# A hybrid decoder layer in split fp32r products: the moving operand read from two halves in turn

## The chip, the cores and the metric

The kernel runs on one core of a Trainium2 chip. A core has a matrix engine (TensorE, PE in the profile, with its weight loads as PEld), a vector engine (VectorE, DVE), a scalar engine (ScalarE, ACT), GpSimd (POOL) and SyncE (SP), which here only issues transfers. Operands lie in SBUF, 128 partitions wide; TensorE writes its sums to PSUM, in banks of 128 x 512 float32. The metric is the device time of one execution in microseconds (us); lower is better.

## The reference

One layer on 256 tokens of width 2048, in float32: a SwiGLU feed-forward block, a mixer with gated linear attention and dilated attention, and a second feed-forward block.

```python
x = x + 0.5 * swiglu(rms_norm(x, ffn1_norm), w_gate, w_up, w_down)        # d_ff = 5632
z = rms_norm(x, mix_norm) @ w_in                                          # split among the head groups
o_g = gla_chunked(...)        # 4 heads, chunks of 64, low-rank forget gate, rms norm and silu gate
o_a = dilated_attention(...)  # 8 heads of 128, three causal dilated windows, merged by softmax
x = x + concat(o_g, o_a) @ w_out
x = x + 0.5 * swiglu(rms_norm(x, ffn2_norm), w_gate2, w_up2, w_down2)

def swiglu(x, w_gate, w_up, w_down):
    return (silu(x @ w_gate) * (x @ w_up)) @ w_down
```

Nearly all the arithmetic is in the dense products with the weights: 2048 x 11264 and 5632 x 2048 twice, 2048 x 6160 for the mixer's input, 2048 x 2048 for its output.

## The kernel before

Each dense product is worked in *column pairs*: two blocks of 512 output columns (`j` = 0, 1) for both halves of the tokens (`t` = 0, 1), so four sums, each in one PSUM bank (`acc`, 6 banks). The loop in `column_pair` goes over the inner dimension in steps `k` of 128. In a step the activations are the stationary operand (128 x 128, loaded anew for each product) and a weight tile of 128 x 512 is the moving operand, which streams through the array.

Weights come from HBM as tiles of 1 MB (`raw`, issued on SP's queue, L148), two steps in each. `split` (L89, L90) turns a step's 128 x 1024 weights into two fp32r tiles: ScalarE writes the rounded value `wh`, VectorE the remainder `wl`. Activations are kept in such halves as well (`hh`/`hl` for the normed input, `uh`/`ul` for the hidden layer, `oah`/`oal` and `ogh`/`ogl` for the mixer's output). `products` then adds three products for each `t` and `j`: high x high (L164), high x low (L166), low x high (L168). A weight step is thus read by 12 products. Four buffers each of `wh` and `wl` are there; ScalarE may overwrite one when the products that read it have ended.

After the last step, `evac(t, ps)` reads the two banks of a token half out of PSUM. In the feed-forward blocks this is a Silu with a per-token scale on ScalarE (`sg`, L218) and a multiplication on VectorE (`u`, L219); `u` is then transposed on TensorE (L85, into a `tp` bank) and split into `uh` and `ul`. The down products and the mixer's output add into the residual `xs` on VectorE (L234, L557), after which the norm of the next part follows in pieces (`norm_block`, `stat_block`), taken from the list `later` and strewn among the next column pair's steps. The mixer's input columns are copied out by ScalarE (L346, L472, L473, L544). The low-rank gate (`gate_low`, L425 to L427) has products of 256 columns of its own and doesn't use `products`. The order on each engine is set by the framework's scheduler from the order of the program.

Transposes, the attention and the gated linear attention run between the steps of column pairs.

Of the kernel before, what the change touches and what calls it, by code (L numbers as in the profile page):

```python
# [17 lines left out]
AF = mybir.ActivationFunctionType  # L18
ALU = mybir.AluOpType
# [17 lines left out]
def layer_kernel(tc, x, xT, gains, gla_gate_up, gla_gate_bias, gla_out_norm, att_q_norm, att_k_norm,  # L37
                 w_ff1, w_dn1, w_mix, w_low, w_out, w_ff2, w_dn2, c_sq, c_rope, c_mask, out):

    nc = tc.nc  # L40
# [3 lines left out]
    with ExitStack() as es:  # L44
# [5 lines left out]
        def acc_bank():  # L50
            return pacc.tile([P, 512], F32, name="acc", tag="acc")

        def t512(name):
            return cst.tile([P, 512], F32, name=name, tag="t512", bufs=4)

        def tp_bank():
            return ptp.tile([P, 512], F32, name="tp", tag="tp")
# [10 lines left out]
        rt = cst.tile([P, NT], F32, name="rt")  # L68
        rq = cst.tile([P, 48], F32, name="rq")[:, :NT]
# [13 lines left out]
        def transpose(dst, src):  # L83
            n = src.shape[0]
            nc.tensor.transpose(dst, src, ident[:n, :n])  # L85

        def split(dst_h, dst_l, src):

            nc.scalar.activation(dst_h, src, AF.Copy)  # L89
            nc.vector.tensor_sub(dst_l, src, dst_h.bitcast(F32))  # L90
# [62 lines left out]
        def weights():  # L153
            while jobs and len(ready) <= AHEAD:
                prepare()
            return ready.pop(0)

        def products(ps, t, acts, ws, first, last, js=((0, 1),)):
            for jj in js:
                for i, ((ah, al, k), (wh, wl)) in enumerate(zip(acts, ws)):  # L160
                    sh = ah[:, k, t * P:(t + 1) * P]
                    sl = al[:, k, t * P:(t + 1) * P]
                    for j in jj:
                        nc.tensor.matmul(ps[j], lhsT=sh, rhs=wh[:, j, :], start=first and i == 0, stop=False)  # L164
                    for j in jj:
                        nc.tensor.matmul(ps[j], lhsT=sh, rhs=wl[:, j, :], start=False, stop=False)  # L166
                    for j in jj:
                        nc.tensor.matmul(ps[j], lhsT=sl, rhs=wh[:, j, :], start=False, stop=last and i == len(ws) - 1)  # L168

        later = []  # L170

        def run_later(n):
            for _ in range(min(n, len(later))):
                later.pop(0)()

        def column_pair(acts, evac, span=28, due=None, extra=None, final=False):

            ps = [None] * NT
            n = len(acts)
            total = done = 0
            i = 0
            while i < n:
                if i == due:
                    done += len(later)
                    run_later(len(later))
                if extra and i in extra:  # L190
                    extra[i]()
                g = WBUF if final and i == n - WBUF else 1
                ws = [weights() for _ in range(g)]
                for t in range(NT):
                    step = 2 * i + t
                    total = max(total, done + len(later))
                    go = max(-(-total * min(step + 1, span) // span) - done, 0)
                    done += min(go, len(later))
                    run_later(go)
                    if i == 0:  # L200
                        ps[t] = [acc_bank(), acc_bank()]
                    last = i + g == n
                    products(ps[t], t, acts[i:i + g], ws, i == 0, last, ((0,), (1,)) if g > 1 else ((0, 1),))
                    if last:
                        evac(t, ps[t])
                i += g

        hacts = [(hh, hl, k) for k in range(KT)]
# [2 lines left out]
        def ffn(name, done, extra=None, final=False):  # L211
            with tc.tile_pool(name=name, bufs=1, reuse_waits="tile") as fp:
                uh = fp.tile([P, FT, S], F32R, name="uh")
                ul = fp.tile([P, FT, S], F32R, name="ul")
                for b in range(FF // 512):
                    def evac(t, ps, b=b):
                        sg, u = t512("sg"), t512("u")
                        nc.scalar.activation(sg, ps[0], AF.Silu, scale=rt[:, t:t + 1])  # L218
                        nc.vector.scalar_tensor_tensor(u, ps[1], rt[:, t:t + 1], sg, op0=ALU.mult, op1=ALU.mult)  # L219
                        tb = tp_bank()  # L220
                        for j in range(4):
                            transpose(tb[:, j * P:(j + 1) * P], u[:, j * P:(j + 1) * P])
                        split(uh[:, 4 * b:4 * b + 4, t * P:(t + 1) * P], ul[:, 4 * b:4 * b + 4, t * P:(t + 1) * P],
                              tb.rearrange("p (j q) -> p j q", j=4))
                    if b:
                        column_pair(hacts, evac)
                    else:
                        column_pair(hacts, evac, span=16, due=15 if extra else 8, extra=extra)
                for cp in range(2):
                    def evac(t, ps, cp=cp):  # L230
                        for j in range(2):
                            c = 2 * cp + j
                            blk = xs[:, t, c * 512:(c + 1) * 512]
                            nc.vector.scalar_tensor_tensor(blk, ps[j], 0.5, blk, op0=ALU.mult, op1=ALU.add)  # L234
                            done(t, c, blk)
                    column_pair([(uh, ul, k) for k in range(FT)], evac, final=final and cp == 1)

# [19 lines left out]
        def renorm(t, c, gi):  # L257

            later.append(lambda: norm_block(t, c, gi))
            later.append(lambda: stat_block(t, c))  # L260
            if c == 3:
                later.append(lambda: norm_finish(t))
# [8 lines left out]
        with tc.tile_pool(name="mix", bufs=1, reuse_waits="tile") as mp:  # L271
# [69 lines left out]
            def store(dst, after=None):  # L341

                def f(t, ps):
                    for j in range(2):
                        blk = dst[:, t, j * 512:(j + 1) * 512]
                        nc.scalar.activation(blk, ps[j], AF.Copy, scale=rt[:, t:t + 1])  # L346
                        if after:
                            later.append(lambda blk=blk, j=j: after(t, j, blk))
                return f
# [63 lines left out]
            def t4k(name):  # L413
                return mp.tile([P, NT, 512], F32, name=name, tag=name, bufs=1)

            qg, kg, la, e1, e2, e3 = (t4k(n) for n in ("qg", "kg", "la", "e1", "e2", "e3"))
# [52 lines left out]
                nc.vector.tensor_mul(kg[:, t, :], kg[:, t, :], er)  # L469

            def evac_qk(t, ps):
                nc.scalar.activation(qg[:, t, :], ps[0], AF.Copy, scale=rq[:, t:t + 1])  # L472
                nc.scalar.activation(kg[:, t, :], ps[1], AF.Copy, scale=rt[:, t:t + 1])  # L473

            column_pair(hacts, evac_qk, span=32)

            vg, on = big("vg"), big("on")
# [53 lines left out]
            def gated(t, j, sg):  # L531
                v = lambda a: a.rearrange("p (h d) -> p h d", h=2)
                nc.vector.tensor_mul(v(sg), v(sg), gon.unsqueeze(1).to_broadcast([P, 2, GDV]))
                nc.vector.tensor_mul(sg, sg, onv[:, t, j * 512:(j + 1) * 512])
                tb = tp_bank()
                for i in range(4):
                    transpose(tb[:, i * P:(i + 1) * P], sg[:, i * P:(i + 1) * P])
                split(oghv[:, 4 * j:4 * j + 4, t * P:(t + 1) * P], oglv[:, 4 * j:4 * j + 4, t * P:(t + 1) * P],
                      tb.rearrange("p (j q) -> p j q", j=4))

            def evac_r(t, ps):
                for j in range(2):
                    sg = t512("sg")
                    nc.scalar.activation(sg, ps[j], AF.Silu, scale=rt[:, t:t + 1])  # L544
                    later.append(lambda j=j, sg=sg: gated(t, j, sg))

            for h in range(GH):
                later.append(lambda h=h: gla_head(h))
            column_pair(hacts, evac_r)

            oacts = [(oah, oal, k) for k in range(8)] + [(oghv, oglv, k) for k in range(8)]
            for cp in range(2):
                def evac(t, ps, cp=cp):
                    for j in range(2):
                        c = 2 * cp + j
                        blk = xs[:, t, c * 512:(c + 1) * 512]
                        nc.vector.tensor_add(blk, blk, ps[j])  # L557
                        renorm(t, c, 2)
                column_pair(oacts, evac, span=4, due=8 if cp == 0 else None)

# [80 lines left out]
```

## Time and profile before

| | |
|---|---|
| median of 3 runs | 1882.87 us (1882.58 to 1882.98) |
| profiled execution | 1883.92 us, its span 1882.0 us |
| TensorE busy | 1871.7 us (99%), 8462 products and transposes |
| TensorE weight loads | 1542.8 us (82%), beside the products |
| VectorE busy | 971.8 us (52%) |
| ScalarE busy | 844.1 us (45%) |
| GpSimd busy | 28.3 us (2%) |
| DMA | 353.79 MB, mean 188 GB/s |
| mean granted TensorE clock | 0.998 |

A group row of the profile reads: line, engine, operation, result<-operands, shapes (partitions x elements per partition), count | busy us, mean ns of one | idle time of the engine before them and what ended it. A row in order of time reads: start, duration (of all that are merged into the row), engine, line, operation, and in brackets the idle time before it. A row of waits reads: who waited for whom, us in total, times, the longest. A row by stretch gives the window, then for each engine its busy time with the number of instructions, then the granted clock and the DMA's share and rate. Products overlap in the array, so the duration of one is longer than the distance between the starts of two.

### The profile page before, as it was taken

What the parts mean: (1) busy time and instruction counts of PE and PEld (TensorE: products, weight loads), DVE (VectorE), ACT (ScalarE), POOL (GpSimd) and SP (SyncE); (2) the same over time, 40 slices, a digit from 0 to 9 for tenths busy, and PEclk for the clock granted to TensorE, in tenths of its full rate; (3) what the DMA queues carried; (4) which work ended last, traced back from release to release, by engine and by line L of the source; (5) the groups of instructions that cost most, each with busy time, mean ns of one, the idle gap of its engine ahead of it and who ended that gap; (6) DMA issues with size and microseconds to landing.
All of it is one profiled execution on the core that took longest, in us unless ns stands there. A gap on an engine that the chain in (4) does not pass through costs nothing.

```text
span 1882.0 us, 20806 instructions
## 1 busy us (share of the span) xinstructions
PE 1871.7 (99%) x8462; PEld 1542.8 (82%) x8462; DVE 971.8 (52%) x998; ACT 844.1 (45%) x1012; POOL 28.3 (2%) x34
## 2 busy tenths in 40 slices
PE   8999999999999999999999999999999999999999
PEld 7888888888888888888887788888888888888887
DVE  5444544554444545566655555444444544544543
ACT  6444444444433434554753444444444444443332
POOL 0000000000000001011000000000000000000000
PEclk9999999999999999999999999999999999999999
DMA  8555555555555555555444355555555555555653
GB/s 314 185 196 182 198 180 199 180 182 198 191 190 200 179 201 196 187 193 185 157 157 149 142 179 187 193 184 196 181 199 180 200 181 197 182 200 183 221 198 115
DMA packets 52111, 353.79 MB, mean 188 GB/s; under 512 B 5904, under 2 KB 7952, under 8 KB 9776
## 3 DMA queue, kind: packets, MB, share of 16 engines
q1 hardware_dynamic: 48672, 348.15, 51.6%
q10 hardware_dynamic: 2896, 3.17, 0.5%
q0 software_dynamic: 448, 1.15, 0.2%
q8 instruction: 66, 1.08, 0.2%
q14 instruction: 29, 0.24, 0.0%
HBM read 350.35 MB, written 2.10 MB: 187 GB/s over the span
## 4 chain that ended last, share of the span: by engine, by line
PE 99%; ACT 1%; DMA 0%; issue 0%; DVE 0%; ACTq 0%
PE acc L164 32%; PE acc L168 32%; PE acc L166 32%; PE tp L85 2%; PE tp L505 0%; DMA xt<-in_xT_dram 0%; PE tp L371 0%; PE tp L520 0%; PE tp L523 0%; ACT wh L89 0%; ACT L438 0%; PE acc L427 0%; PE acc L426 0%; PE acc L425 0%; PE tp L434 0%
## 5 line engine op out<-in xcount | busy, mean ns | idle before, releaser
L90 DVE TENSOR_TENSOR wl<-raw,wh 128x1024 fp32r<-128x1024 f32 x658 | 803.6, 1225 | 765.6 <-ACT wh L89 765.1
L89 ACT ACTIVATE wh<-raw 128x1024 fp32r<-128x1024 f32 x658 | 694.7, 1060 | 862.5 <-PE acc L168 852.7
L166 PE MATMUL acc<-wl,hh 128*128 128x512 f32 x1792 | 568.7, 392 | 0.0
L168 PE MATMUL acc<-wh,hl 128*128 128x512 f32 x1792 | 563.3, 391 | 0.0
L164 PE MATMUL acc<-wh,hh 128*128 128x512 f32 x1792 | 558.0, 392 | 4.4 <-ACT wh L89 4.4
L164 PEld LDWEIGHTS acc<-wh,hh 128*128 128x128 f32 x1792 | 336.7, 188 | 74.7 <-ACT wh L89 4.7
L168 PEld LDWEIGHTS acc<-wh,hl 128*128 128x128 f32 x1792 | 336.3, 188 | 71.3 <-issue 2.1
L166 PEld LDWEIGHTS acc<-wl,hh 128*128 128x128 f32 x1792 | 336.3, 188 | 70.6 <-issue 2.0
L166 PE MATMUL acc<-wl,uh 128*128 128x512 f32 x704 | 220.0, 389 | 0.0
L168 PE MATMUL acc<-wh,ul 128*128 128x512 f32 x704 | 219.1, 389 | 0.0
L164 PE MATMUL acc<-wh,uh 128*128 128x512 f32 x704 | 218.3, 390 | 0.0
L166 PEld LDWEIGHTS acc<-wl,uh 128*128 128x128 f32 x704 | 132.1, 188 | 27.4
L168 PEld LDWEIGHTS acc<-wh,ul 128*128 128x128 f32 x704 | 132.1, 188 | 27.3
L164 PEld LDWEIGHTS acc<-wh,uh 128*128 128x128 f32 x704 | 132.1, 188 | 27.3
L90 DVE TENSOR_TENSOR ul<-tp,uh 128x512 fp32r<-128x512 f32 x44 | 30.0, 691 | 69.5 <-ACT uh L89 69.5
L89 ACT ACTIVATE uh<-tp 128x512 fp32r<-128x512 f32 x44 | 26.3, 599 | 84.9 <-PE tp L85 83.3
L218 ACT ACTIVATE sg<-acc,rt 128x512 f32<-128x512 f32 x44 | 30.4, 690 | 16.4 <-PE acc L168 14.7
L219 DVE SCALAR_TENSOR_TENSOR u<-acc,rt,sg 128x512 f32<-128x512 f32 x44 | 32.9, 748 | 5.3 <-ACT sg L218 5.3
L85 PE MATMUL tp<-ident,u 128*128 128x128 f32 x176 | 26.4, 272 | 0.0
L85 PEld LDWEIGHTS tp<-ident,u 128*128 128x128 f32 x176 | 21.9, 141 | 4.4
L106 POOL TENSOR_TENSOR rs<-a,mhalf 128x4 f32<-128x4 f32 (+1 forms) x12 | 17.5, 1455 | 292.2 <-DVE a L321 292.2
L164 PE MATMUL acc<-wh,oah 128*128 128x512 f32 x64 | 21.0, 396 | 0.0
(147 smaller groups left out, 561.8 us busy)
## 6 DMA issues: line engine op xcount, KB each, us to landing
raw<-in_w_ff_dram SPq DMA_DIRECT2D x175, 1024.0 KB, 4.8
raw<-in_w_dn_dram SPq DMA_DIRECT2D x88, 1024.0 KB, 4.7
raw<-in_w_mix_dram SPq DMA_DIRECT2D x48, 1024.0 KB, 4.8
raw<-in_w_out_dram SPq DMA_DIRECT2D x16, 1024.0 KB, 4.8
xt<-in_xT_dram ACTq DMA_DIRECT2D x8, 256.0 KB, 8.0
xs<-in_x_dram SPq DMA_DIRECT2D x2, 1024.0 KB, 9.8
raw<-in_w_ff_dram SPq DMA_DIRECT2D x4, 256.0 KB, 5.8
raw<-in_w_low_dram SPq DMA_DIRECT2D x1, 1024.0 KB, 4.8
```

Source lines behind the costliest of these rows:

```text
L85: nc.tensor.transpose(dst, src, ident[:n, :n])
L89: nc.scalar.activation(dst_h, src, AF.Copy)
L90: nc.vector.tensor_sub(dst_l, src, dst_h.bitcast(F32))
L106: nc.gpsimd.tensor_tensor(dst, src, mhalf[:, :src.shape[-1]], op=ALU.pow)
L164: nc.tensor.matmul(ps[j], lhsT=sh, rhs=wh[:, j, :], start=first and i == 0, stop=False)
L166: nc.tensor.matmul(ps[j], lhsT=sh, rhs=wl[:, j, :], start=False, stop=False)
L168: nc.tensor.matmul(ps[j], lhsT=sl, rhs=wh[:, j, :], start=False, stop=last and i == len(ws) - 1)
L218: nc.scalar.activation(sg, ps[0], AF.Silu, scale=rt[:, t:t + 1])
L219: nc.vector.scalar_tensor_tensor(u, ps[1], rt[:, t:t + 1], sg, op0=ALU.mult, op1=ALU.mult)
```

## The change

Two helpers give other views of the same memory. `alt` lets the 512 columns of a weight tile be read as column 0, 256, 1, 257, ..., 255, 511. The sums therefore stand in PSUM in that order, written one after the other as before. Where they are read out, `column_pair` hands the evacuation each bank in a view that takes the even words first and then the odd ones (2 runs of 256 with a step of two), and `halves` gives the result the matching two runs, which follow one another, so that every result lies where it did. The weight splits, the transfers, the stationary operands, the gate's 256-column products, the transposes and the order of the instructions on each engine are the same; lines behind the helpers have numbers higher by 7 (L164 is L171, L166 is L173, L168 is L175, L218 is L225, L219 is L226).

```diff
+        def alt(a):
+
+            return a.rearrange("p (b a) -> p a b", b=2)
+
+        def halves(a):
+            return a.rearrange("p (b a) -> p b a", b=2)
+
         def products(ps, t, acts, ws, first, last, js=((0, 1),)):
...
                     for j in jj:
-                        nc.tensor.matmul(ps[j], lhsT=sh, rhs=wh[:, j, :], start=first and i == 0, stop=False)
+                        nc.tensor.matmul(ps[j], lhsT=sh, rhs=alt(wh[:, j, :]), start=first and i == 0, stop=False)
                     for j in jj:
-                        nc.tensor.matmul(ps[j], lhsT=sh, rhs=wl[:, j, :], start=False, stop=False)
+                        nc.tensor.matmul(ps[j], lhsT=sh, rhs=alt(wl[:, j, :]), start=False, stop=False)
                     for j in jj:
-                        nc.tensor.matmul(ps[j], lhsT=sl, rhs=wh[:, j, :], start=False, stop=last and i == len(ws) - 1)
+                        nc.tensor.matmul(ps[j], lhsT=sl, rhs=alt(wh[:, j, :]), start=False, stop=last and i == len(ws) - 1)
...
                     if last:
-                        evac(t, ps[t])
+                        evac(t, [b.rearrange("p (a b) -> p b a", b=2) for b in ps[t]])
...
-                        nc.scalar.activation(sg, ps[0], AF.Silu, scale=rt[:, t:t + 1])
-                        nc.vector.scalar_tensor_tensor(u, ps[1], rt[:, t:t + 1], sg, op0=ALU.mult, op1=ALU.mult)
+                        nc.scalar.activation(halves(sg), ps[0], AF.Silu, scale=rt[:, t:t + 1])
+                        nc.vector.scalar_tensor_tensor(halves(u), ps[1], rt[:, t:t + 1], halves(sg), op0=ALU.mult, op1=ALU.mult)
...
-                            nc.vector.scalar_tensor_tensor(blk, ps[j], 0.5, blk, op0=ALU.mult, op1=ALU.add)
+                            nc.vector.scalar_tensor_tensor(halves(blk), ps[j], 0.5, halves(blk), op0=ALU.mult, op1=ALU.add)
...
-                        nc.vector.tensor_add(blk, blk, ps[j])
+                        nc.vector.tensor_add(halves(blk), halves(blk), ps[j])
```

The other evacuations (L346, L472, L473, L544) take `halves` in the same way.

More of the change, by code (lines that the diff above doesn't have):

```diff
@@ L345, in f @@
                         blk = dst[:, t, j * 512:(j + 1) * 512]
-                        nc.scalar.activation(blk, ps[j], AF.Copy, scale=rt[:, t:t + 1])
+                        nc.scalar.activation(halves(blk), ps[j], AF.Copy, scale=rt[:, t:t + 1])
                         if after:
@@ L471, in evac_qk @@
             def evac_qk(t, ps):
-                nc.scalar.activation(qg[:, t, :], ps[0], AF.Copy, scale=rq[:, t:t + 1])
-                nc.scalar.activation(kg[:, t, :], ps[1], AF.Copy, scale=rt[:, t:t + 1])
+                nc.scalar.activation(halves(qg[:, t, :]), ps[0], AF.Copy, scale=rq[:, t:t + 1])
+                nc.scalar.activation(halves(kg[:, t, :]), ps[1], AF.Copy, scale=rt[:, t:t + 1])
             column_pair(hacts, evac_qk, span=32)
@@ L543, in evac_r @@
                     sg = t512("sg")
-                    nc.scalar.activation(sg, ps[j], AF.Silu, scale=rt[:, t:t + 1])
+                    nc.scalar.activation(halves(sg), ps[j], AF.Silu, scale=rt[:, t:t + 1])
                     later.append(lambda j=j, sg=sg: gated(t, j, sg))
```

## The prediction

> **What bounds the kernel now.** I read the head of the page first, then the chain that ended last, then the stretches in time, then the costliest groups. Head and chain:
>
> ```profile
> span 1882.0 us, 20806 instructions
> PE 1871.7 (99%) x8462; PEld 1542.8 (82%) x8462; DVE 971.8 (52%) x998; ACT 844.1 (45%) x1012; POOL 28.3 (2%) x34
> ...
> PE 99%; ACT 1%; DMA 0%; issue 0%; DVE 0%; ACTq 0%
> PE acc L164 32%; PE acc L168 32%; PE acc L166 32%; PE tp L85 2%; PE tp L505 0%; DMA xt<-in_xT_dram 0%; PE tp L371 0%; PE tp L520 0%; PE tp L523 0%; ACT wh L89 0%; ACT L438 0%; PE acc L427 0%; PE acc L426 0%; PE acc L425 0%; PE tp L434 0%
> ```
>
> TensorE is the chain from end to end, and 96% of it are the three lines of `products`. Next, whether it ever waits inside (waits of all engines, and busy time by stretch):
>
> ```profile
> ACT wh L89 <- PE acc L168: 852.7, 545, 5.1
> DVE wl L90 <- ACT wh L89: 765.1, 574, 4.1
> ...
> PE acc L164 <- ACT wh L89: 4.4, 1, 4.4
> ```
>
> ```profile
> 11.00:14.00 3.00, 3.00 (x8) 2.32 (x8) 2.28 (x4) 1.58 (x4) 0.00 (x0) 0.50 1.01 417
> ...
> 1205.00:1645.00 440.00, 440.00 (x1982) 364.78 (x1982) 219.39 (x197) 190.10 (x199) 0.00 (x0) 1.00 0.53 191
> ```
>
> TensorE waits once, 4.4 us at the start. Everyone else waits for it: ScalarE 852.7 us before it may overwrite a weight buffer, VectorE behind ScalarE. In the second window TensorE is busy 440.00 of 440.00 us at clock 1.00. So whatever one product gains or loses is paid in full, and whatever VectorE, ScalarE or a DMA loses is paid only past their slack.
>
> How many products there are, by shape:
>
> ```profile
> L89 ACT ACTIVATE wh<-raw 128x1024 fp32r<-128x1024 f32 x658 | 694.7, 1060 | 862.5 <-PE acc L168 852.7 <-issue 6.3 <-PE acc L426 2.6
> L166 PE MATMUL acc<-wl,hh 128*128 128x512 f32 x1792 | 568.7, 392 | 0.0
> L166 PE MATMUL acc<-wl,uh 128*128 128x512 f32 x704 | 220.0, 389 | 0.0
> L166 PE MATMUL acc<-wl,oah 128*128 128x512 f32 x64 | 20.6, 393 | 0.0
> L166 PE MATMUL acc<-wl,ogh 128*128 128x512 f32 x64 | 19.7, 389 | 0.0
> ```
>
> L166 has 1792+704+64+64 = 2624. The three lines run alike, so 7872 products; and 658 weight splits less the 2 for the low-rank gate, times 2 token halves, 2 column blocks and 3 products, are 7872 too. The 392 ns are the latency of one; they overlap. Their spacing is read from starts (order of time, TensorE; first and last of 77 rows with two products each, so 76 steps of two):
>
> ```profile
> 23.63 0.62 PE L166 MATMUL acc<-wl,hh 128*128 128x512 f32 x2
> ...
> 58.08 0.61 PE L168 MATMUL acc<-wh,hl 128*128 128x512 f32 x2
> ```
>
> 34.45 us / 152 = 226.6 ns per product. The products of the low-rank gate have 256 columns and the same weight type (first and last of 46 in a row, 45 steps):
>
> ```profile
> 878.93 0.28 PE L427 MATMUL acc<-hh,wl 128*128 128x256 f32 x1
> ...
> 884.33 0.28 PE L427 MATMUL acc<-hh,wl 128*128 128x256 f32 x1
> ```
>
> 5.40 / 45 = 120.0 ns. So a column costs (226.6 - 120.0) / 256 = 0.416 ns, 512 of them 213.2 ns, and 13.4 ns are a fixed gap. [...] One more row says what a column costs when it comes at half that pace, in the window above where the clock was 0.50:
>
> ```profile
> 12.01 1.05 PE L168 MATMUL acc<-wh,hl 128*128 128x512 f32 x2
> 12.86 1.05 PE L166 MATMUL acc<-wl,hh 128*128 128x512 f32 x2
> 13.71 1.05 PE L168 MATMUL acc<-wh,hl 128*128 128x512 f32 x2
> ```
>
> 1.70 us for four: 425 ns, 0.83 ns per column, with the gap gone.
>
> **The change, part by part.** Nothing is added or taken away: the same rows stand in the same order on all five engines, so no wait, transfer or queue is moved. Two access patterns differ.
>
> *The moving read.* Column i of the array's stream was word i of a row of 512; now it is word 0, 256, 1, 257 and so on, each read 1 KB away from the last. No row of this trace reads a moving operand other than word after word, so the price is bounded. From below: nothing, or the loss of the 13.4 ns gap if reading in two places hides it (-105 us). [...] I quote ScalarE's and VectorE's copies out of PSUM at two widths:
>
> ```profile
> L90 DVE TENSOR_TENSOR ul<-tp,uh 128x512 fp32r<-128x512 f32 x44 | 30.0, 691 | 69.5 <-ACT uh L89 69.5
> L89 ACT ACTIVATE uh<-tp 128x512 fp32r<-128x512 f32 x44 | 26.3, 599 | 84.9 <-PE tp L85 83.3
> ...
> L90 DVE TENSOR_TENSOR oal<-tp,oah 128x256 fp32r<-128x256 f32 x8 | 3.4, 419 | 0.4 <-ACT oah L89 0.3
> L89 ACT ACTIVATE oah<-tp 128x256 fp32r<-128x256 f32 x8 | 3.0, 381 | 3.6 <-PE tp L397 3.5
> ```
>
> ScalarE: (599 - 381) / 256 = 0.85 ns per word. VectorE: (691 - 419) / 256 = 1.06 ns. The cold products (0.83) and ScalarE (0.85) agree on about 0.83 ns for one word alone; TensorE at full clock is the only engine here that takes two words in that time, which it can do as long as the two are neighbours. I take this value: a column at 0.83 ns, that is 213.2 ns more per product. I keep the gap of 13.4 ns: it vanished in the cold rows because the array was slower than the read, and now the read is the slower. Sum: 7872 products less the 14 that started before 15 us at half clock (there a column already takes 0.83 ns) = 7858; x 213.2 ns = 1675 us on the path, all of it, since TensorE never waits. The weight loads keep their pattern and still fit beside (82% busy now, less then).
>
> [...]
>
> *The evacuations.* 68 on ScalarE and 68 on VectorE now read words 8 bytes apart; their results are still written in sequence. These are their commonest rows, and one such place in order of time:
>
> ```profile
> L219 DVE SCALAR_TENSOR_TENSOR u<-acc,rt,sg 128x512 f32<-128x512 f32 x44 | 32.9, 748 | 5.3 <-ACT sg L218 5.3
> L218 ACT ACTIVATE sg<-acc,rt 128x512 f32<-128x512 f32 x44 | 30.4, 690 | 16.4 <-PE acc L168 14.7
> ```
>
> ```profile
> 55.85 0.69 ACT L218 ACTIVATE sg<-acc,rt 128x512 f32<-128x512 f32 x1 [0.67 <-PE acc L168]
> ```
>
> ```profile
> 56.57 0.75 DVE L219 SCALAR_TENSOR_TENSOR u<-acc,rt,sg 128x512 f32<-128x512 f32 x1 [0.30 <-ACT sg L218]
> ```
>
> ```profile
> 60.58 0.60 PE L85 MATMUL tp<-ident,u 128*128 128x128 f32 x4
> ```
>
> Bounds: nothing, or one more step per word, 512 x 0.85 = 0.44 us on ScalarE and 512 x 1.06 = 0.54 us on VectorE. [...] Even at the upper end the second `u` ends at 57.32 + 0.44 x 2 + 0.54 = 58.7 us, and the transposes that need it start at 60.58, behind products of the next pair: covered by 1.8 us, and by more if products are slower. The other kind of place is the residual block, whose norm transposes follow:
>
> ```profile
> 1146.23 0.69 DVE L557 TENSOR_TENSOR xs<-xs,acc 128x512 f32<-128x512 f32 x1 [1.54 <-PE acc L168]
> 1147.97 1.88 DVE L557 TENSOR_TENSOR xs<-xs,acc 128x512 f32<-128x512 f32 x3
> ```
>
> ```profile
> 1150.80 0.60 PE L85 MATMUL tp<-ident,xs 128*128 128x128 f32 x4
> ```
>
> The first block is ready at 1146.92 and is transposed at 1150.80; an added 0.54 us is covered there by 3.3 us. Were that cover gone everywhere, 68 x 0.44 + 68 x 0.54 = 67 us; that is only an upper end. The very last addition (L234) is exposed, at most 0.54 us.
>
> Sum: the profiled execution took 1883.92 us (span 1882.0), 1.05 above the median of 1882.87. 1883.92 + 1675 - 1 = 3558 us. The range of this case: gap lost as well (199.8 ns per product, 1570 us) 3453; whole spacing doubled (226.6 ns, 1781 us) and all evacuations exposed 3731.
>
> **The rivals.**
>
> *Free: the read keeps up.* Each half is itself read in order. If the read path holds the last piece of both halves, or reads far enough ahead, every second access meets a piece already fetched, and 512 columns still need no more fetches than now. It decides at 213.2 ns for 512 words: below that TensorE does not see it. [...] Against it: the read then must serve two places in 0.83 ns without slack. Time 1883 us, within 0.2% of before, which is about what a measurement of this kernel can tell from no change. The case in which the built pattern is joined back into one run of 512 gives this time too. Chance 0.22. The gain that it might bring, 13.4 ns x 7858 = 105 us if the gap goes too, ends at 1778: 0.02.
>
> [...] VectorE's pace of 1.06 ns would give 544 ns, 2600 us more, about 4480. Chance of this group, all above 3731: 0.20. [...]
>
> *In part.* Some hops pay, half of them for instance: 106.6 ns x 7858 = 838 us, 2721. Nothing in the trace speaks for a fraction; all between 1.02 and 1.8 times: 0.12.
>
> **How the numbers follow.** Twice the column time 0.44, free 0.22, faster 0.02, in part 0.12, more than twice 0.20. The point is the likeliest, 3558, its own range 3453 to 3731. The range for 8 in 10 leaves out the group above 3731, and so begins at the free case: 1877 (1883 less half of what a measurement tells, rounded) to 3731. Faster 0.02, same 0.22, slower 0.76.
>
> **What would show it.** [...] The gate's 256-column products, which are not touched, must stay at 120.0 ns, and the transposes of `u` likewise; the PSUM reads at 690 and 748 ns. TensorE should still be 99% busy at clock 1.00 while VectorE and ScalarE fall to about a quarter. I am wrong if the spacing stays at 227, or if TensorE now waits for `u` or for a PSUM bank, or if the clock drops because the array idles between columns.

## The result, and the profile after

The changed kernel takes 1795.83 us (median of 4 runs, 1795.65 to 1795.99) against 1882.92 us for the kernel before: a ratio of 0.9537, 95% interval 0.9521 to 0.9554. It is 87 us faster. I had forecast 3558 us.

The head of the page after, and the chain that ended last:

```profile
span 1794.0 us, 20802 instructions
PE 1783.4 (99%) x8462; PEld 1553.0 (87%) x8462; DVE 970.2 (54%) x998; ACT 840.6 (47%) x1012; POOL 28.2 (2%) x34
...
PE 99%; ACT 1%; DMA 0%; DVE 0%; issue 0%; ACTq 0%
```

TensorE is still the chain, with 88 us less of it. The same stretch as before the change, in which TensorE was busy 440.00 of 440.00 us:

```profile
1205.00:1645.00 440.00, 440.00 (x2076) 385.63 (x2075) 228.55 (x203) 196.18 (x204) 0.00 (x0) 1.00 0.56 200
```

It holds 2076 products and transposes where it held 1982, at the same clock of 1.00. So each product takes less time; no wait went, since there was none. Their spacing (order of time, TensorE; first and last of 37 rows of two products, 36 steps of two):

```profile
29.82 0.59 PE L175 MATMUL acc<-wh,hl 128*128 128x512 f32 x2
...
45.36 0.59 PE L175 MATMUL acc<-wh,hl 128*128 128x512 f32 x2
```

15.54 us / 72 = 215.8 ns, where it was 226.6. 10.8 ns x 7858 products = 85 of the 87 us. The gate's products, whose read was not changed (first and last of the 16 of L434, 45 steps):

```profile
837.13 0.28 PE L434 MATMUL acc<-hh,wl 128*128 128x256 f32 x1
...
842.53 0.28 PE L434 MATMUL acc<-hh,wl 128*128 128x256 f32 x1
```

5.40 / 45 = 120.0 ns, as before. And the evacuations that read PSUM in steps of two words (costliest groups):

```profile
L225 ACT ACTIVATE sg<-acc,rt 128x512 f32<-128x512 f32 x44 | 30.2, 687 | 14.0 <-PE acc L175 13.4
L226 DVE SCALAR_TENSOR_TENSOR u<-acc,rt,sg 128x512 f32<-128x512 f32 x44 | 32.9, 747 | 2.8 <-ACT sg L225 0.4
```

687 and 747 ns after, 690 and 748 before: the steps cost nothing.

At a granted clock of 0.50 the changed kernel takes 1.71 us for four products (11.86 to 13.57 us), 427 ns each, where the kernel before took 425. So half the clock still gives about twice the 213.2 ns that 512 columns take at full clock, and what shrank is what a product takes beyond that, 13.4 to 2.6 ns.

### The profile page after: what moved, and what is told of

Same layout as the page of the kernel before. It is cut to its first block, busy times and chain, and to the rows that moved or that the text cites. A ratio compares the mean times of both kernels' runs of the same rounds, so it can differ in the third digit from the quotient of the medians.

```text
span 1794.0 us, 20802 instructions
## 1 busy us (share of the span) xinstructions
PE 1783.4 (99%) x8462; PEld 1553.0 (87%) x8462; DVE 970.2 (54%) x998; ACT 840.6 (47%) x1012; POOL 28.2 (2%) x34
## 4 chain that ended last, share of the span: by engine, by line
PE 99%; ACT 1%; DMA 0%; DVE 0%; issue 0%; ACTq 0%
PE acc L171 32%; PE acc L173 31%; PE acc L175 31%; PE tp L85 2%; PE tp L512 0%; DMA xt<-in_xT_dram 0%; PE tp L378 0%; PE tp L527 0%; PE tp L530 0%; ACT wh L89 0%; ACT L445 0%; PE acc L432 0%; PE acc L433 0%; PE acc L434 0%; PE tp L404 0%
## 5 line engine op out<-in xcount | busy, mean ns | idle before, releaser
L173 PE MATMUL acc<-wl,hh 128*128 128x512 f32 x1792 | 549.2, 382 | 0.0
L175 PE MATMUL acc<-wh,hl 128*128 128x512 f32 x1792 | 543.9, 380 | 0.0
L171 PE MATMUL acc<-wh,hh 128*128 128x512 f32 x1792 | 538.5, 382 | 4.3 <-ACT wh L89 4.3
L171 PEld LDWEIGHTS acc<-wh,hh 128*128 128x128 f32 x1792 | 339.0, 190 | 52.8 <-ACT wh L89 4.6
L175 PEld LDWEIGHTS acc<-wh,hl 128*128 128x128 f32 x1792 | 338.6, 189 | 49.1 <-issue 2.1
L173 PEld LDWEIGHTS acc<-wl,hh 128*128 128x128 f32 x1792 | 338.6, 189 | 49.0 <-issue 2.0
L173 PE MATMUL acc<-wl,uh 128*128 128x512 f32 x704 | 212.6, 379 | 0.0
L175 PE MATMUL acc<-wh,ul 128*128 128x512 f32 x704 | 211.8, 379 | 0.0
L171 PE MATMUL acc<-wh,uh 128*128 128x512 f32 x704 | 210.8, 380 | 0.0
L175 PEld LDWEIGHTS acc<-wh,ul 128*128 128x128 f32 x704 | 133.1, 189 | 18.8
L173 PEld LDWEIGHTS acc<-wl,uh 128*128 128x128 f32 x704 | 133.1, 189 | 18.8
L171 PEld LDWEIGHTS acc<-wh,uh 128*128 128x128 f32 x704 | 133.0, 189 | 18.7
L225 ACT ACTIVATE sg<-acc,rt 128x512 f32<-128x512 f32 x44 | 30.2, 687 | 14.0 <-PE acc L175 13.4
L226 DVE SCALAR_TENSOR_TENSOR u<-acc,rt,sg 128x512 f32<-128x512 f32 x44 | 32.9, 747 | 2.8 <-ACT sg L225 0.4
L171 PE MATMUL acc<-wh,oah 128*128 128x512 f32 x64 | 20.2, 385 | 0.0
```

Of the source, the lines that this page charges most:

```text
L171: nc.tensor.matmul(ps[j], lhsT=sh, rhs=alt(wh[:, j, :]), start=first and i == 0, stop=False)
L173: nc.tensor.matmul(ps[j], lhsT=sh, rhs=alt(wl[:, j, :]), start=False, stop=False)
L175: nc.tensor.matmul(ps[j], lhsT=sl, rhs=alt(wh[:, j, :]), start=False, stop=last and i == len(ws) - 1)
L225: nc.scalar.activation(halves(sg), ps[0], AF.Silu, scale=rt[:, t:t + 1])
L226: nc.vector.scalar_tensor_tensor(halves(u), ps[1], rt[:, t:t + 1], halves(sg), op0=ALU.mult, op1=ALU.mult)
```

## The experiments

Two questions: why did a read that hops 1 KB at every word not cost, and where did the gap go? Each kernel below was run once, beside a run of the kernel before on the same chip (1883.3 to 1883.8 us; all runs of that kernel lie between 1882.6 and 1883.9). The effects are tens of us or more except where noted. Spacings are worked out as above.

### Other hops: steps of two, sixteen places, pairs

`e1_step2` and `e2_hop16` are the changed kernel with another number of places (256 runs of two words, read word by word across; and 16 runs of 32):

```diff
-            return a.rearrange("p (b a) -> p a b", b=2)
+            return a.rearrange("p (b a) -> p a b", b=256)   # e2: b=16
```

with the views of PSUM and results to match. `e3_pairs` reads 0, 1, 256, 257, 2, 3, ...:

```diff
+            return a.rearrange("p (b a c) -> p a b c", b=2, c=2)
```

> The weight tile is read in steps of two words (the 256 even columns, then the 256 odd ones), 8 bytes from one word to the next; the evacuation puts the columns back in order. Theory A (a stream whose neighbours are adjacent words pays 13.4 ns between products, any other pays 2.5): products start every 215.7 ns, 1796 us. Theory B (the gain needs two places far apart in the memory): 226.6 ns or more, 1883 us or more. Theory C (any pattern of more than one dimension is started sooner): 215.7 ns, 1796 us.

> The tile is read in 16 places in turn, 128 bytes from one word to the next. A and C: 215.7 ns, 1796 us, as with two places. B, if the number of places or their distance matters (two pieces can be held, sixteen can't): over 226.6 ns, up to 427 ns, 1883 to 3500 us.

> Two adjacent words of the lower half, then two of the upper half, and so on; the evacuation is as before the change, so the columns stay in that order (the undoing is left out). A: half of the neighbours are adjacent; if adjacency of words is what costs, 226.6 ns and 1883 us. B and C: 215.7 ns, 1796 us.

Measured: 3645.38, 3517.14 and 2701.67 us. In order of time, steps of two words (5 steps of two products), 16 places (5 steps) and pairs (24 rows, 23 steps):

```profile
399.99 1.08 PE L171 MATMUL acc<-wh,hh 128*128 128x512 f32 x2
...
404.50 1.08 PE L175 MATMUL acc<-wh,hl 128*128 128x512 f32 x2
```

```profile
399.98 1.06 PE L173 MATMUL acc<-wl,hh 128*128 128x512 f32 x2
...
404.33 1.06 PE L171 MATMUL acc<-wh,hh 128*128 128x512 f32 x2
```

```profile
30.06 0.84 PE L167 MATMUL acc<-wh,hh 128*128 128x512 f32 x2
...
45.40 0.83 PE L171 MATMUL acc<-wh,hl 128*128 128x512 f32 x2
```

451, 435 and 333 ns. In e2's trace the granted clock is 0.50 from 11 to 14 us, and four products take 1.74 us there too (11.92 to 13.66), 435 ns each: the same spacing at half clock as at full clock, where the kernel before takes 425 and 226.6. So hops can cost just what I forecast, about twice the time, and the two places in turn of the change do not. Theory A (words that are not adjacent are quick) falls by e1 and e2, C (any pattern of two dimensions) by e1 and e2 too. B fits e1 (and e2 but for 8 ns over its upper value), but not the pairs, which are as far apart as in the change and cost half as much again. The pairs gave the clue. There the words in even positions of the stream are 0, 256, 2, 258; in the change they are 0, 1, 2, 3.

### One product kind alone

`e4_low_only`: only L166's read is in turn from two halves; its tile is written in the order that undoes it.

```diff
-            split(wh, wl, raws[0][:, k])
+            nc.scalar.activation(wh, raws[0][:, k], AF.Copy)
+            v = lambda a: a.rearrange("p j (a b) -> p j a b", b=2)
+            nc.vector.tensor_sub(wl.rearrange("p j (b a) -> p j a b", b=2), v(raws[0][:, k]), v(wh.bitcast(F32)))
...
-                        nc.tensor.matmul(ps[j], lhsT=sh, rhs=wl[:, j, :], start=False, stop=False)
+                        nc.tensor.matmul(ps[j], lhsT=sh, rhs=alt(wl[:, j, :]), start=False, stop=False)
```

> Only the products with the low half of the weights (L171 here, two of six) read in turn from two halves; the split writes that tile so that the columns come in their order, and the evacuation is as before the change. Every theory in which a product pays at its own start or end: two of six intervals are 10.9 ns shorter, 2624 x 10.9 ns = 29 us, 1854 us; which interval (the one before or the one behind such a product) says whether the gap is at its start or its end. If the gap is in the evacuation or elsewhere in the program: 1883 us.

Measured 1880.06 us, a miss for each theory that adds up: 3.7 us less than the kernel before beside it, where 29 were expected. Order of time:

```profile
400.02 0.62 PE L169 MATMUL acc<-wh,hh 128*128 128x512 f32 x2
400.49 0.59 PE L171 MATMUL acc<-wl,hh 128*128 128x512 f32 x2
400.92 0.63 PE L173 MATMUL acc<-wh,hl 128*128 128x512 f32 x2
401.38 0.62 PE L169 MATMUL acc<-wh,hh 128*128 128x512 f32 x2
```

L171 takes 0.43 us for two, as in the changed kernel, but L169 and L173 take 0.46 to 0.47, not 0.453: six products take 1.36 us, as before the change. The gain of the quick products was lost again in their neighbours. The run changes one thing more, VectorE's writes of `wl`, which now hop and take longer (2035 ns in place of 1225). They are not the reason: in this trace 459 steps from one plain product to the next fell wholly into time in which VectorE ran nothing, and they took 231.2 ns on the mean, against 226.6 before the change. The 11 ns are thus no fixed price of the product that pays it. Why the neighbours pay stays open. Apart from its start, TensorE also waits 3.8 us for VectorE in this run, against 0.2 us before the change.

### Where the even and the odd positions read

Theory P, formed after e3: the array takes two words at a time, one for the even and one for the odd position of the stream; each of the two is quick while its own words are neighbours. Four runs test it. `e7_hop4` has four places in turn (b=4). `e8_blocks` alternates between the two column blocks, 2 KB apart. `e11_alternate_step2` alternates, but takes every second word on each side. `e12_near` alternates between 8 words and the 8 words behind them:

```diff
+ e8:   rhs=wh[:, :, 256 * j:256 * j + 256].rearrange("p b a -> p a b")
+ e11:  rhs=wh.rearrange("p u f -> p (u f)").rearrange("p (b a u) -> p u a b", b=2, u=2)[:, j]
+ e12:  rhs=wh[:, j, :].rearrange("p (c b a) -> p c a b", b=2, a=8)
```

(and the same for `wl`).

> Four places in turn, 512 bytes apart. Theory P (the array takes two words at a time, one for the even and one for the odd position of the stream, and each of the two is quick only while its own words are neighbours): each of the two now goes to and fro between two runs, as in the read by pairs, so 333 ns or more, 2700 us or more. Theory L (a few pieces last fetched are held, more than two): 215.7 ns, 1796 us.

> A product takes the lower (or the upper) 256 columns of both column blocks in turn, so the two places lie 2 KB apart instead of 1 KB; the columns are left in that order. If the distance of the two places doesn't matter (P and L): 215.7 ns, 1796 us. If the two must fall into different parts of the memory by their distance: another value, up to 435 ns and 3520 us.

> Two places in turn, but in each every second word: word 0, 512, 2, 514, ... of the 1024 words of both blocks; the columns are left in that order. [...] Theory C (a pattern of two dimensions, or of two words per turn, is quick by itself): 215.8 ns, 1796 us. [...]

> Two places in turn that lie side by side: word 0, 8, 1, 9, ..., 7, 15, then 16, 24, ...; 32 bytes apart; the columns are left in that order. Theory P: even and odd positions each run through words that are neighbours, 215.8 ns, 1796 us. If two long runs or far apart places are needed: 226.6 ns or more.

Measured: 2322.78, 1795.23, 1883.39 and 1794.54 us. First and last rows of two in the same stretch, for e7 (27 steps of two), e11 (35 steps) and e12 (37 steps):

```profile
29.89 0.73 PE L171 MATMUL acc<-wh,hh 128*128 128x512 f32 x2
...
45.19 0.73 PE L171 MATMUL acc<-wh,hh 128*128 128x512 f32 x2
```

```profile
29.85 0.61 PE L169 MATMUL acc<-wl,hh 128*128 128x512 f32 x2
...
45.72 0.62 PE L167 MATMUL acc<-wh,hh 128*128 128x512 f32 x2
```

```profile
29.68 0.59 PE L171 MATMUL acc<-wh,hl 128*128 128x512 f32 x2
...
45.65 0.59 PE L167 MATMUL acc<-wh,hh 128*128 128x512 f32 x2
```

283, 226.7 and 215.8 ns. e8 has the first and the last of 37 rows at 29.94 and 45.48 us, 215.8 ns as well. All nine patterns together:

| stream | words at even positions | ns per product |
|---|---|---|
| after; e8; e12 | 0, 1, 2, 3 | 215.8 |
| before | 0, 2, 4, 6 | 226.6 |
| e11: 0, 512, 2, 514 | 0, 2, 4, 6 | 226.7 |
| e7: 0, 128, 256, 384, 1 | 0, 256, 1, 257 | 283 |
| e3: 0, 1, 256, 257, 2 | 0, 256, 2, 258 | 333 |
| e2: 0, 32, 64, 96 | 0, 64, 128, 192 | 435 |
| e1: 0, 2, 4, 6 | 0, 4, 8, 12 | 451 |

The middle column sorts the times into steps of one word, of two words, and all that goes further; the distance from one word of the stream to the next does not. e11 beside e8 is the sharpest: both alternate between places 2 KB apart, and only the step on each side differs, one word (215.8) or two (226.7, the spacing of the plain read). e12 shows that the places need not be far apart. Among the slow patterns P gives no order: in e7, e3, e2 and e1 alike each word at an even position lies four words or more from the one before it, and they range from 283 to 451 ns. For e7 it said 333 ns or more and missed, at 283. These times are measured, not explained, and that the array takes two words at a time is inferred from the table; no trace shows it directly. L said 215.7 for e7 and falls.

### Where the gap comes from

Theory S held that the gap is what the weight load's fetches, which run beside, take from a moving read that has no room to spare. `e5_stationary` (kernel before) and `e9_both` (changed kernel) let the load step by two words:

```diff
-                    sh = ah[:, k, t * P:(t + 1) * P]
+                    sh = ah[:, k, :].rearrange("p (i u) -> p u i", u=2)[:, t, :]
```

(the same for `sl`). `e10_narrow_load` cuts the load of L166 to 64 columns (`ps[j][:64, :]`, `sh[:, :64]`); `e13_load_one_word` reads one word 128 times (`to_broadcast`); `e14_load_step4` and `e15_both_step4` step by four words over two inner steps, before and after the change.

> The moving read is as before the change, word after word; the stationary operand is read in steps of two words (even tokens for t = 0, odd ones for t = 1; the rows are left in that order). Theory S (the 11 ns are a collision between the moving read and the weight load, both word after word): the spacing moves away from 226.6 ns, to 216 at best, 1796 us. Theory M (the gap belongs to the moving read alone): 226.6 ns, 1883 us.

> The changed kernel (moving read from two halves in turn) with the stationary operand in steps of two words, as in the run that did this to the kernel before; the rows are left in the order of even and odd tokens. Theory S with slack (moving read and weight load get in each other's way, and a read from two halves has room to make that good): 215.8 ns as without it, 1796 us. Theory of a dearer weight load that is paid whatever the moving read does: 215.8 + 6.8 = 222.6 ns, 1849 us.

> The kernel before, but in the products high x low (L166, two of six) the stationary operand has 64 columns in place of 128 (the other half of these products is left out), so that the weight load beside the moving read is half as long. Theory S: the intervals in which such a load runs have half the gap, about 220 ns, 2624 x 6.7 ns = 17 us less in all, 1866 us. Theory M (the gap belongs to the moving read alone): 226.6 ns in all, 1883 us.

> [...] Theory S (the gap is what the weight load's fetches take from a moving read without slack): the gap all but goes, 216 to 219 ns, 1796 to 1825 us. Theory M (the gap belongs to the moving read alone): 226.6 ns, 1883 us.

> [...] Theory M with a cost of the step of two for another reason: 226.6 to 233.4 ns.

> The changed kernel with the same weight load in steps of four words. If the read from two halves has room for all the load's fetches: 215.8 ns, 1796 us. [...]

Measured: 1932.17, 1795.43, 1905.23, 1910.93, 1958.70 and 1974.09 us. Order of time for e5 (35 rows of two, 34 steps) and e9 (37 rows, 36 steps):

```profile
29.87 0.63 PE L168 MATMUL acc<-wh,hl 128*128 128x512 f32 x2
...
45.74 0.63 PE L164 MATMUL acc<-wh,hh 128*128 128x512 f32 x2
```

```profile
29.92 0.59 PE L175 MATMUL acc<-wh,hl 128*128 128x512 f32 x2
...
45.46 0.59 PE L175 MATMUL acc<-wh,hl 128*128 128x512 f32 x2
```

15.87 / 68 = 233.4 ns for the plain read, 15.54 / 72 = 215.8 for the read from two halves. The same dearer load costs the one 6.8 ns and the other nothing. That much of S is shown, and theory M (the moving read alone) falls: the plain read's gap depends on the load beside it. But how is not what S said. A load half as wide (e10, 134 ns per load in place of 188) and a load of a single word (e13, 189 ns) should have shortened the gap, and both lengthened it (75 rows of two each, 74 steps):

```profile
23.62 0.61 PE L166 MATMUL acc<-wl,hh 128*64 128x512 f32 x2
...
57.66 0.62 PE L164 MATMUL acc<-wh,hh 128*128 128x512 f32 x2
```

```profile
23.73 0.62 PE L168 MATMUL acc<-wh,hl 128*128 128x512 f32 x2
...
57.61 0.62 PE L166 MATMUL acc<-wl,hh 128*128 128x512 f32 x2
```

230.0 and 228.9 ns on the mean, both misses; over the whole run they lost 22 and 27 us, 2.8 and 3.5 ns per product. So a smaller load does not make the gap shorter. Neither run shows what is fetched, and both change more than that (the width of a product's result in e10, a repeated word in e13). The steps of four words missed as well: e14 lies above what M allowed, e15 above the 1796 us of a read that has room. They don't answer the question, since the load itself became the bound (by stretch, e14; third field PEld):

```profile
1205.00:1645.00 440.00, 440.00 (x1904) 438.67 (x1903) 213.19 (x192) 183.22 (x190) 0.00 (x0) 1.00 0.51 183
```

Weight loads are busy 438.67 of 440.00 us there, in e15 438.87. e15's 1974 us are therefore no evidence against the room that e9 shows. What sets the length of the plain read's gap stays open; that it varies with the load, and that the read from two halves keeps 215.8 ns under both loads that leave the load itself off the bound, is measured.

### Once per product or per column

`e6_gate` reads the gate's 256 columns from two halves as well (`rhs=alt(hh[:, k, :])` and so on, with `halves` where the result is copied).

> The changed kernel, with the 48 products of the gate (256 columns) read from two halves as well. If the 10.9 ns are saved once per product: their spacing falls from 120.0 to 109.1 ns. If they are saved per column: 114.5 ns. The total would fall by 0.5 or 0.3 us, too little to be seen in the time.

Measured 1794.94 us, 0.9 below the changed kernel's median, too little to be told from nothing with one run. The gate's products (16 rows of L434, 45 steps):

```profile
836.48 0.28 PE L434 MATMUL acc<-hh,wl 128*128 128x256 f32 x1
...
841.50 0.28 PE L434 MATMUL acc<-hh,wl 128*128 128x256 f32 x1
```

5.02 / 45 = 111.6 ns: 8.4 saved of the 13.4 there, about midway between the two forecasts. So the saving is neither a fixed amount per product nor one per column, and the split of a product into a price per column and a fixed gap is only a rough account: between the two widths, both read from two halves, it gives (215.8 - 111.6) / 256 = 0.407 ns for a column, less than the 0.416 of the plain reads. No run was quicker than the changed kernel by more than 1.3 us (e12).

## Why the prediction was wrong

- *What bounds the kernel*: right. TensorE never waited, and each ns on a product came out times 7858.
- *The price of a column under the hop*: this is the step that failed. I took 0.83 ns, "for one word alone; TensorE at full clock is the only engine here that takes two words in that time, which it can do as long as the two are neighbours". The two words need not be neighbours of each other (215.8 ns in the change, where none are). What counted in the runs is where each lies against the word two positions earlier: next to it in the change, two words on in the plain read (226.6 ns, and 226.7 in e11). In the change the price of the hop is nothing. Where the word two positions earlier lies four words away or more on one run (e1, e2), 435 to 451 ns came out, near my 426 to 440. That does not bear out the mechanism that I gave, since by it the pairs' stream, half of whose neighbours are adjacent, would cost less than four places in turn, and it cost more (333 against 283).
- *The gap of 13.4 ns*: a term that failed as well. "I keep the gap", because the read would be the slower side; it went to 2.6 ns. The runs show that the plain read's gap moves with the load beside it (226.6 to 233.4 ns in e5) and that the read from two halves keeps 215.8 ns under the same load (e9); what sets its length they leave open. I had a row that pointed there: at half clock, where the read had twice the time, the gap was gone. I had put the loss of the gap at 105 us with a chance of 0.02; it measured 87.
- *Free because each half is read in order*: the rival at 0.22 named the right property of the stream, and stopped at no gain.
- *The evacuations*: right, at nothing (687 and 747 ns after, 690 and 748 before). That is measured for reads of PSUM in steps of two words; VectorE's writes to SBUF in e4 did pay for a hop (2035 ns in place of 1225).
- *More than twice, at 0.20*: no run shows such a price. The dearest read, in e1, took 451 ns per product and 3645.38 us in all, below the 3731 at which this group began.
- *The order of instructions, transfers, the gate's 120.0 ns, the clock*: unchanged, as said.

## What to carry to other kernels

Before pricing an access pattern by its largest hop, write down what the even and the odd positions of the stream read, each by itself: with fp32r operands, neighbours there ran at 215.8 ns for 512 columns, every second word at 226.6, every fourth at 451. A gap that is gone where the stream has twice the time, as here at half clock, is worth a forecast of its own as something to be gained. If such a read is tried, change all the products of a loop: in the one run with two of six changed, the gain went back to the neighbours.

## What was not expected of the hardware

- A moving read that alternates between two places, 32 bytes, 1 KB or 2 KB apart, beats the plain one by 10.8 ns per product of 512 fp32r columns.
- The plain read's spacing moves with the weight load beside it: 226.6 ns as is, 233.4 with steps of two words, 228.9 with a single word, 230.0 with two loads of six at half width.
- VectorE's split in e4, which writes with a hop of 1 KB at each word, took 2035 ns for 1024 columns against 1225 when it writes in order:

```profile
L152 DVE TENSOR_TENSOR wl<-raw,wh 128x1024 fp32r<-128x1024 f32 x656 | 1319.5, 2035 | 312.1 <-ACT wh L150 311.7
```
